# Pacing the modulation-weight chunks of a four-layer hybrid model: other breakpoints in the table that spreads them over the projection chunks

## Chip, cores and metric

One core of a Trainium2 chip runs the whole program. The metric is device time in microseconds (us) of one execution, and the median over several executions is what counts. The granted clock of TensorE (PE) has two levels, 1.2 and 2.4 GHz; the profile gives it as a share of the upper one.

## What is computed

Four layers act on a sequence of 256 tokens of width 2048. Each layer is modulated by a vector that depends only on `c`, and its weights are large: 2048 x 6144 floats per layer.

```python
c_act = jax.nn.silu(c)
for i in range(DEPTH):                      # 4 layers
    mod = jnp.einsum('bd,de->be', c_act, ada_w[i]) + ada_b[i]
    shift, scale, gate = jnp.split(mod[:, None, :], 3, axis=-1)
    h = rms_normalize(x, norm_g[i], NORM_EPS) * (1 + scale) + shift
    ...                                     # layers 0 and 3: rwkv7_mixer, 1: gla_mixer, 2: ssd_mixer
    x = x + (gate * out).astype(x.dtype)
return rms_normalize(x, final_g, NORM_EPS)
```

Each mixer is one wide input projection (cut into several parts), a recurrence over heads in chunks, and an output projection.

## The kernel before

**Projections.** All projections go through `jobs` (L359 and on). A projection of 256 output columns is cut into *weight chunks* of 512 KB (four 128-row slices of 256 columns; the output projection of a RWKV layer also has chunks of two slices). For each weight chunk SP issues one DMA into a tile `raw` (L348), ScalarE (ACT) casts it into `H` (L338), VectorE (DVE) subtracts to get the rest `L` (L340), and PE runs 24 matmuls of 256 columns with it (L393): high x high, high x low and low x high. After each weight chunk `tick()` is called.

**Modulation.** The first layer's shift and scale are made at the start. The other ten thirds (layer 0's gate, then shift, scale and gate of layers 1 to 3) are made by the generator `ada_third` in 320 *modulation chunks*, 32 to a third. Each is one DMA of 512 KB into a tile `raw` and one DVE operation of 128 x 1024 elements that multiplies and adds it into `adaacc` (L304). Both kinds of chunk share the six `raw` buffers and the SP queue: SP waits, in order, until a buffer is free.

**Pacing.** `tick()` counts the weight chunks (`tk`, 670 in all) and reads from the table `PACE` how many modulation chunks should have been asked for by now. It asks for at most two per tick. During the last column block of a layer's output projection, and the first jobs of the next layer, `hold` is set and none is asked for. Where a layer needs a third that isn't complete, `ada_need` asks for all that is missing at once.

```python
n = min(int(np.interp(self.tk, *PACE)), self.paced + 2)
if not self.hold:
    self.ada_tick(n - self.paced)
    self.paced = n
```

`tk` is 144 at the end of layer 0, 276 at the end of layer 1, 502 at the end of layer 2 and 670 at the end. Layer 1 can't start before 97 modulation chunks have been asked for, layer 2 before 193, layer 3 before 289.

**Order.** A scheduler places the instructions of each engine when the program is built; each engine then runs its own in that order. In a RWKV layer the stages are: V projection, K projection (with `rwkv_first` for eight units of heads: elementwise work and the inverse of small triangular blocks through `bd`, `dx`, `dt`, mostly on DVE), R projection (with `rwkv_second`), G projection, and the output projection in three parts: units 0 to 3, units 4 to 6, and unit 7, whose weight chunks are half as large. "Out 1" below are the first 24 weight chunks of it, "Out 2" the last 16.

Of the kernel before, what the change touches and what calls it, by code (L numbers as in the profile page):

```python
# [92 lines left out]

RAWC = 1024

PACE = ((0, 60, 78, 150, 319, 530, 660), (0, 0, 16, 96, 234, 292, 320))

SHARE = (1, 0, 1, 0, 1, 0, 1, 0)

# [30 lines left out]
class Kern:  # L130
# [264 lines left out]
    def tick(self):  # L395

        self.tk += 1
        n = min(int(np.interp(self.tk, *PACE)), self.paced + 2)
        if not self.hold:
# [1066 lines left out]
```

## Time and profile before

| | us |
|---|---|
| median of 3 runs | 2886.83 |
| lowest and highest run | 2881.13, 2887.49 |
| profiled execution | 2881.41 |
| its span, first to last instruction | 2879.4 |
| PE busy | 2691.4 |
| DVE busy | 2213.7 |
| ACT busy | 1392.7 |

A row of windows of the profile gives the busy time of each engine in a stretch of the execution; length minus busy time is the engine's idle time there. The stretches used below begin where ACT casts the first weight chunk of a stage:

| stage | us from the span's start |
|---|---|
| layer 0: K, R, G | 199.7, 340.6, 490.8 |
| layer 0: Out 1, Out 2 | 660.8, 805.1 |
| layer 1 (gla): its first 24 weight chunks, then the next 96 | 866.8, 963.3 to 1281.5 |
| layer 2 (ssd): group 0; group 1 to its gate part; to the end of the first output block | 1352.3, 1408.3, 1491.8 |
| layer 2: the next 56 weight chunks; the 56 after them | 1613.3, 1789.4 |
| end of layer 2 and start of layer 3 | 2042.2 to 2158.7 |
| layer 3: K, R, G | 2227.4, 2372.7, 2522.8 |
| layer 3: Out 1, Out 2 | 2695.6, 2823.4 to 2853.6 |

### The profile page before, as it was taken

To read this page: it belongs to the slowest core of one execution; us is meant where nothing else is said; L and a number is where in the kernel's file an instruction comes from. 1 tells how busy PE (TensorE), PEld (TensorE's weight loads), DVE (VectorE), ACT (ScalarE), POOL (GpSimd) and SP (SyncE) were. 2 spreads that over 40 slices of the span, in tenths; PEclk is the share of its full clock that TensorE was granted. 3 is DMA by queue.
4 is the path that set the end of the run, shared out by engine and by line. 5 is a ranking of instruction groups with operands and counts; after the bars stand their busy time and mean duration, and the time that the engine had idled before them with its cause. 6 is when DMAs were issued, how large, how long until landed. Compare 5 with 4: busy or idle time off the path is not lost.

```text
span 2879.4 us, 62022 instructions
## 1 busy us (share of the span) xinstructions
PE 2691.4 (93%) x25074; PEld 2533.2 (88%) x25074; DVE 2213.7 (77%) x3918; ACT 1392.7 (48%) x2315; POOL 153.8 (5%) x298
## 2 busy tenths in 40 slices
PE   6899899999977999998998999999889989999997
PEld 4789899998967899987898999999779989899997
DVE  5778777878788988877888787887678888565666
ACT  3475655333335544444544454554357666452333
POOL 0011110101000000000000000000001011110100
PEclk8899889999998999999999999999999989999999
DMA  9876558978586888975775767666557765684633
GB/s 341 313 239 198 165 162 285 352 270 293 178 287 222 315 296 295 321 257 196 280 264 191 233 221 232 220 212 223 180 170 242 228 197 184 194 299 160 206 118 114
DMA packets 239118, 673.55 MB, mean 234 GB/s; under 512 B 72272, under 2 KB 78416, under 8 KB 235760
## 3 DMA queue, kind: packets, MB, share of 16 engines
q1 hardware_dynamic: 217904, 580.84, 59.8%
q0 software_dynamic: 20928, 88.75, 8.6%
q8 instruction: 197, 3.23, 0.5%
q14 instruction: 89, 0.73, 0.1%
HBM read 620.66 MB, written 48.82 MB: 233 GB/s over the span
## 4 chain that ended last, share of the span: by engine, by line
PE 72%; DVE 10%; DMA 10%; issue 3%; ACT 2%; SPq 2%; POOL 0%; DVEq 0%; ACTq 0%; POOLq 0%
PE acc L393 56%; DMA raw<-in_ada_w 3%; DVE L L340 3%; PE g L785 2%; PE pv L393 2%; DVE adaacc L304 2%; ACT H L338 1%; DMA raw<-in_rwkv_w_in 1%; DMA raw<-in_rwkv_w_out 1%; DMA dx<-bd 1%; PE b L892 1%; PE b L869 1%; DMA raw<-in_gla_w_in 1%; PE b L891 1%; PE b L864 1%
## 5 line engine op out<-in xcount | busy, mean ns | idle before, releaser
L393 PE MATMUL acc<-xs,H 128*128 128x256 f32 x8480 | 1631.3, 291 | 32.0 <-ACT H L338 8.4
L393 PEld LDWEIGHTS acc<-xs,H 128*128 128x128 f32 x8480 | 1359.7, 196 | 61.7 <-ACT H L338 10.9
L393 PE MATMUL acc<-xs,L 128*128 128x256 f32 x4240 | 1228.9, 290 | 18.2 <-DVE L L340 17.9
L338 ACT CAST H<-raw 128x1024 fp32r<-128x1024 f32 (+1 forms) x706 | 718.2, 1018 | 862.0 <-PE acc L393 636.1
L340 DVE TENSOR_TENSOR L<-raw,H 128x1024 fp32r<-128x1024 f32 (+1 forms) x706 | 834.1, 1184 | 249.0 <-ACT H L338 233.9
L393 PEld LDWEIGHTS acc<-xs,L 128*128 128x128 f32 x4240 | 828.3, 195 | 31.9 <-DVE L L340 23.4
L304 DVE SCALAR_TENSOR_TENSOR adaacc<-raw,cact,adaacc 128x1024 f32<-128x1024 f32 x300 | 384.0, 1280 | 111.5 <-DMA raw<-in_ada_w 109.5
L393 PE MATMUL acc<-ys,H 128*128 128x256 f32 x1536 | 292.2, 290 | 10.1 <-DVE ys L409 3.8
L393 PEld LDWEIGHTS acc<-ys,H 128*128 128x128 f32 x1536 | 244.7, 194 | 20.7 <-issue 7.4
L393 PE MATMUL acc<-ys,L 128*128 128x256 f32 x768 | 221.1, 288 | 0.0
L393 PEld LDWEIGHTS acc<-ys,L 128*128 128x128 f32 x768 | 149.0, 194 | 3.2 <-issue 3.2
L551 ACT ACTIVATE hn<-x,mod,omu 128x256 f32<-128x256 f32 x192 | 113.4, 599 | 2.9 <-DVE xm L554 1.4
L431 DVE SCALAR_TENSOR_TENSOR x<-acc,mod,x 128x256 f32<-128x256 f32 x192 | 83.7, 478 | 33.3 <-PE acc L393 33.1
L393 PE MATMUL acc<-H,xs 128*128 128x256 f32 x512 | 97.4, 290 | 0.9 <-ACT vt L1072 0.7
L554 DVE SCALAR_TENSOR_TENSOR xm<-x,par,hn 128x256 f32<-128x256 f32 x192 | 88.9, 478 | 1.4 <-ACT hn L551 0.3
L393 PEld LDWEIGHTS acc<-H,xs 128*128 128x128 f32 x512 | 82.7, 198 | 2.5 <-issue 1.2
L393 PE MATMUL acc<-L,xs 128*128 128x256 f32 x256 | 73.7, 289 | 0.0
L785 PE MATMUL g<-abkp 64*128 64x128 f32 x768 | 68.6, 294 | 1.8 <-DVE abkp L807 1.7
L408 ACT CAST xs<-xm 128x256 fp32r<-128x256 f32 x128 | 50.9, 400 | 34.1 <-DVE xm L554 31.8
L785 PEld LDWEIGHTS g<-abkp 64*128 64x128 f32 x768 | 53.4, 189 | 14.2 <-issue 6.2
L1278 DVE SCALAR_TENSOR_TENSOR cva<-cvp,hcw,cva 128x256 f32<-128x256 f32 x144 | 65.1, 478 | 0.0
L278 DVE SCALAR_TENSOR_TENSOR adaacc<-raw,cact,adaacc 128x512 f32<-128x512 f32 x56 | 42.0, 749 | 28.1 <-DMA raw<-in_ada_w 23.4
(358 smaller groups left out, 3138.4 us busy)
## 6 DMA issues: line engine op xcount, KB each, us to landing
raw<-in_ada_w SPq DMA_DIRECT2D x384, 512.0 KB, 4.9
raw<-in_rwkv_w_in SPq DMA_DIRECT2D x256, 512.0 KB, 4.8
raw<-in_ssd_w_in SPq DMA_DIRECT2D x128, 512.0 KB, 4.3
raw<-in_gla_w_in SPq DMA_DIRECT2D x96, 512.0 KB, 5.2
raw<-in_ssd_w_out SPq DMA_DIRECT2D x64, 512.0 KB, 4.0
raw<-in_rwkv_w_out SPq DMA_DIRECT2D x48, 512.0 KB, 4.4
abkp<-kd POOLq DMA_DIRECT2D x16, 1024.0 KB, 7.8
raw<-in_gla_w_out SPq DMA_DIRECT2D x32, 512.0 KB, 4.9
```

Of the source, the lines that this page charges most:

```text
L278: nc.vector.scalar_tensor_tensor(out=acc, in0=raw[:, u, :], scalar=self.cact[:, k:k + 1], in1=acc, op0=ALU.mult, op1=ALU.add)
L304: nc.vector.scalar_tensor_tensor(out=acc, in0=raw, scalar=self.cact[:, k:k + 1], in1=acc, op0=ALU.mult, op1=ALU.add)
L338: nc.scalar.copy(out=hi, in_=raw[:, a:a + n])
L340: nc.vector.tensor_tensor(out=lo, in0=raw[:, a:a + n], in1=hi, op=ALU.subtract)
L393: self.nc.tensor.matmul(ps, lhs, rhs, start=first and part == 0 and w is hi, stop=last and w is lo)
L408: nc.scalar.copy(out=t[:, 0, :], in_=src)
L431: nc.vector.scalar_tensor_tensor(out=self.x[:, t, 1:], in0=ps[:, u, :], scalar=gate[:, t:t + 1], in1=self.x[:, t, 1:], op0=ALU.mult, op1=A ...
L551: nc.scalar.activation(t1, x[:, k, 1:], AF.Identity, scale=self.omu[:, col:col + 1], bias=self.mods[(i, 0)][:, k:k + 1])
L554: done[k] = nc.vector.scalar_tensor_tensor(out=xm, in0=x[:, k, 0:T], scalar=self.p("rwkv_mu", col), in1=t1, op0=ALU.mult, op1=ALU.add)
L785: self.nc.tensor.matmul(ps[h][:, n * C:(n + 1) * C], s[r, q, c * C:(c + 1) * C], t[r, q, c * C:(c + 1) * C], start=True, stop=True)
L864: nc.tensor.matmul(ps[:, n * H:(n + 1) * H], G[h][:, q, :], tk[:, 2, q, HS[h]], start=not c, stop=not c or h == 1)
L1278: nc.vector.scalar_tensor_tensor(out=a, in0=src[:, k:k + T], scalar=w[k], in1=a, op0=ALU.mult, op1=ALU.add)
```

## The change

Only the table is changed: its first tuple holds counts of weight chunks, the second the modulation chunks to be asked for by then.

```diff
-PACE = ((0, 60, 78, 150, 319, 530, 660), (0, 0, 16, 96, 234, 292, 320))
+PACE = ((0, 156, 286, 518, 640), (0, 97, 194, 290, 320))
```

The rate in modulation chunks per weight chunk goes from 0 (first 60), 0.89, 1.11, 0.82, 0.27 and 0.22 to 0.62, 0.75, 0.46 and 0.25. Counted in the order in which SP issues the loads of the two programs, the modulation chunks fall so:

| stage (weight chunks in it) | before | after |
|---|---|---|
| layer 0: V (40) | 1 | 5 |
| K (32) | 0 | 20 |
| R (32) | 10 | 20 |
| G (32) | 34 | 20 |
| Out 1 (24) | 27 | 15 |
| Out 2 (16), the forced ones at its end included | 25 | 17 |
| layer 1: first 24 | 22 | 17 |
| next 96 | 79 | 72 |
| last 16 | 12 | 12 |
| layer 2: group 0 and group 1 (16 + 24) | 33 | 19 |
| to the end of the first output block (32) | 9 | 17 |
| the next 56 and 56 and 24 | 15, 15, 7 | 23, 23, 10 |
| end of layer 2 and start of layer 3 (26) | 7 | 11 |
| layer 3: V, K, R, G | 5, 7, 7, 5 | 5, 8, 6, 0 |
| Out 1, Out 2 | 0, 0 | 0, 0 |

The SP queue of the program before, in layer 0 from the last two LoRA loads (`rwkv_dec_w`, `rwkv_iclr_w`) through V's last eight loads into K. `bd` and `dx` are the small transfers of the inverse.

```order
L348 DMA raw<-in_rwkv_dec_w 128x384
L348 DMA raw<-in_rwkv_iclr_w 128x384
L348 DMA raw<-in_rwkv_w_in 128x1024 x25
L924 DMA bd<-LT 16x8x16 x8
L348 DMA raw<-in_rwkv_w_in 128x1024
L927 DMA dx<-bd 64x256
```

The same place in the program after; `in_ada_w` are the modulation chunks.

```order
L348 DMA raw<-in_rwkv_w_in 128x1024 x2
L298 DMA raw<-in_ada_w 128x1024
L348 DMA raw<-in_rwkv_w_in 128x1024
L298 DMA raw<-in_ada_w 128x1024
L348 DMA raw<-in_rwkv_w_in 128x1024 x2
L298 DMA raw<-in_ada_w 128x1024
L348 DMA raw<-in_rwkv_w_in 128x1024 x2
```

Where SP issued 25 weight chunks in a row, it now issues a modulation chunk after every one or two of them.

DVE in the K stage of layer 0 in the program before (`xm` and `xs` are the mixed input of the next projection, `thd` and `abk` belong to `rwkv_first`):

```order
L340 TENSOR_TENSOR L<-raw,H 128x1024 x2
L752 TENSOR_TENSOR thd<-thd,abk 128x512
L754 SCALAR_TENSOR_TENSOR abk<-abk 128x512
L340 TENSOR_TENSOR L<-raw,H 128x1024
L756 SCALAR_TENSOR_TENSOR abk<-abk,bkk 128x256
L758 SCALAR_TENSOR_TENSOR abk<-abk,nkk,Pt 128x256
```

The same work of DVE in the program after:

```order
L304 SCALAR_TENSOR_TENSOR adaacc<-raw,cact,adaacc 128x1024
L340 TENSOR_TENSOR L<-raw,H 128x1024 x2
L752 TENSOR_TENSOR thd<-thd,abk 128x512
L754 SCALAR_TENSOR_TENSOR abk<-abk 128x512
L340 TENSOR_TENSOR L<-raw,H 128x1024
L745 TENSOR_SCALAR n_2538<-b_2533 128x8
L756 SCALAR_TENSOR_TENSOR abk<-abk,bkk 128x256
L758 SCALAR_TENSOR_TENSOR abk<-abk,nkk,Pt 128x256
L756 SCALAR_TENSOR_TENSOR abk<-abk,bkk 128x256
L758 SCALAR_TENSOR_TENSOR abk<-abk,nkk,Pt 128x256
L304 SCALAR_TENSOR_TENSOR adaacc<-raw,cact,adaacc 128x1024
```

The modulation operations (L304) now stand between the `L` of the weight chunks and the work of `rwkv_first`; before, this stage had none.

The SP queue at the end of layer 0's output projection, before (`128x512` are the half chunks of unit 7, `gla_low` is the first load of layer 1):

```order
L348 DMA raw<-in_rwkv_w_out 128x512
L298 DMA raw<-in_ada_w 128x1024 x2
L348 DMA raw<-in_rwkv_w_out 128x512
L298 DMA raw<-in_ada_w 128x1024
L348 DMA raw<-in_rwkv_w_out 128x512
L298 DMA raw<-in_ada_w 128x1024
L348 DMA raw<-in_rwkv_w_out 128x512
L298 DMA raw<-in_ada_w 128x1024 x8
L348 DMA raw<-in_gla_low 128x4x16
```

The same place after:

```order
L348 DMA raw<-in_rwkv_w_out 128x512 x2
L298 DMA raw<-in_ada_w 128x1024
L348 DMA raw<-in_rwkv_w_out 128x512
L298 DMA raw<-in_ada_w 128x1024
L348 DMA raw<-in_rwkv_w_out 128x512 x2
L298 DMA raw<-in_ada_w 128x1024
L348 DMA raw<-in_rwkv_w_out 128x512 x2
L298 DMA raw<-in_ada_w 128x1024 x8
L348 DMA raw<-in_gla_low 128x4x16
```

Fewer modulation chunks stand between the half chunks; the eight that layer 1 forces at the end stand there in both.

## Rows read from the trace of the kernel before

**Rows 1.** The page's head: span, and PE's busy time and share.

```profile
span 2879.4 us, 62022 instructions
...
PE 2691.4 (93%) x25074; PEld 2533.2 (88%) x25074; DVE 2213.7 (77%) x3918; ACT 1392.7 (48%) x2315; POOL 153.8 (5%) x298
```

**Rows 2.** The page's costliest groups, L304: busy us, mean ns of one, idle before.

```profile
L304 DVE SCALAR_TENSOR_TENSOR adaacc<-raw,cact,adaacc 128x1024 f32<-128x1024 f32 x300 | 384.0, 1280 | 111.5 <-DMA raw<-in_ada_w 109.5
```

**Rows 3.** Windows: V's end, K, R, G, Out 1, Out 2, layer 1's start.

```profile
core 0: us, PE busy (x) PEld busy (x) DVE busy (x) ACT busy (x) POOL busy (x), PEclk, DMA share, GB/s
...
150.00:200.00 50.00, 46.30 (x353) 44.70 (x353) 34.63 (x60) 36.02 (x66) 8.96 (x20) 0.93 0.69 232
...
199.70:340.60 140.90, 136.04 (x1509) 129.68 (x1507) 115.67 (x253) 90.88 (x177) 14.93 (x28) 0.98 0.61 190
340.60:490.80 150.20, 144.73 (x2120) 137.17 (x2121) 108.35 (x206) 83.96 (x159) 15.70 (x31) 0.92 0.64 208
490.80:660.80 170.00, 166.78 (x1542) 157.43 (x1541) 137.66 (x214) 65.71 (x106) 19.92 (x37) 1.00 0.87 314
660.80:805.10 144.30, 136.98 (x1182) 128.92 (x1181) 108.66 (x207) 44.88 (x76) 11.76 (x22) 0.96 0.66 228
805.10:866.80 61.70, 43.66 (x292) 34.79 (x292) 54.10 (x78) 20.89 (x40) 0.00 (x0) 0.95 0.87 289
866.80:963.30 96.50, 83.03 (x590) 74.87 (x591) 82.11 (x121) 54.44 (x83) 0.52 (x1) 0.88 0.71 238
```

**Rows 4.** Windows: layer 3's K, G, Out 1, Out 2.

```profile
2227.40:2372.70 145.30, 136.41 (x1358) 128.91 (x1357) 122.12 (x261) 92.90 (x181) 14.89 (x26) 0.95 0.68 220
...
2522.80:2695.60 172.80, 172.05 (x1701) 161.08 (x1700) 103.33 (x183) 65.42 (x108) 19.95 (x37) 1.00 0.63 217
2695.60:2823.40 127.80, 125.89 (x1126) 119.91 (x1125) 88.96 (x191) 43.44 (x74) 11.74 (x22) 1.00 0.49 160
2823.40:2853.60 30.20, 30.20 (x249) 29.03 (x247) 20.61 (x35) 14.19 (x23) 0.00 (x0) 1.00 0.36 119
```

**Rows 5.** Windows of L304 alone: layer 0's G, Out 1, Out 2; layer 3's K, G.

```profile
490.80:660.80 170.00, 42.23 (x33) 1.00 0.87 314
660.80:805.10 144.30, 25.59 (x20) 0.96 0.66 228
805.10:866.80 61.70, 29.43 (x23) 0.95 0.87 289
...
2227.40:2372.70 145.30, 7.68 (x6) 0.95 0.68 220
...
2522.80:2695.60 172.80, 5.10 (x4) 1.00 0.63 217
```

**Rows 6.** Windows of 72 us: in layer 0's G, and in layer 1.

```profile
504.00:576.00 72.00, 69.33 (x618) 65.39 (x616) 57.93 (x90) 26.01 (x41) 10.27 (x19) 1.00 0.96 352
...
936.00:1008.00 72.00, 69.58 (x553) 63.94 (x553) 64.93 (x87) 37.84 (x60) 0.00 (x0) 0.98 0.89 315
```

**Rows 7.** The longest wait in Out 2: us in total, times, longest.

```profile
ACT H L338 <- DMA raw<-in_rwkv_w_out: 25.2, 15, 3.9
```

**Rows 8.** The chain of work that ended last in Out 2, by line.

```profile
by line: DMA raw<-in_rwkv_w_out 33.9%; DVE adaacc L304 18.5%; issue 16.2%; DVE x L431 11.3%; DVE L L340 7.1%; DMA raw<-in_gla_low 5.8%; ACT H L338 5.8%; DVE ylast L680 1.1%; DVE rst L1042 0.3%; DVE ysq L902 0.2%; DVE rsv L1035 0.2%; DVE rst
```

**Rows 9.** Windows: layer 1's middle, layer 2's first stretches, one steady, its end.

```profile
963.30:1281.50 318.20, 311.33 (x2522) 296.04 (x2522) 259.35 (x335) 143.91 (x206) 0.00 (x0) 0.98 0.85 302
...
1352.30:1408.30 56.00, 51.42 (x394) 49.85 (x393) 49.02 (x83) 31.71 (x47) 1.66 (x3) 0.94 0.75 259
1408.30:1491.80 83.50, 79.19 (x658) 76.58 (x657) 74.29 (x128) 41.64 (x59) 0.53 (x1) 0.96 0.85 299
1491.80:1613.30 121.50, 110.02 (x905) 106.07 (x904) 94.96 (x180) 53.70 (x76) 1.06 (x2) 0.94 0.58 196
1613.30:1789.40 176.10, 176.10 (x1497) 172.43 (x1496) 147.25 (x265) 89.39 (x127) 1.06 (x2) 1.00 0.68 225
...
2042.20:2158.70 116.50, 96.69 (x668) 86.76 (x668) 78.33 (x150) 57.05 (x102) 6.87 (x10) 0.88 0.48 159
```

## The prediction

> **What bounds the kernel now.** I read the page first: PE is busy for 93% of the span and DVE for 77% [rows 1], so on the whole this is a PE kernel, and a modulation chunk, which costs no PE time, is free wherever PE has other work and DVE and the queues keep up. What it costs DVE is 1.280 us each [rows 2]; what it costs the DMA engines is 512 KB. Then I cut the span into the stages of the layers and read windows, each engine's busy time against the length. Three kinds of stage come out. In the steady part of layer 2 PE has no idle time at all, with DVE busy for 147.25 of 176.1 us, 0.84 [rows 9]. In the RWKV stages K and R PE is idle for 4.9 and 5.5 us and DVE is busy for 0.82 and 0.72 [rows 3]. And at the seams PE does stand still: 18.0 of 61.7 us in Out 2, 13.5 of 96.5 us at layer 1's start [rows 3], 4.6, 4.3 and 11.5 us in the first three stretches of layer 2 [rows 9], with the granted clock down to 0.88 to 0.96 there. The chain of waits in Out 2 tells what the standstill is made of: a third of it is weight chunks landing, 18.5% modulation operations on DVE [rows 8], and ACT waited 25.2 us for weights [rows 7]. So the question of this change is what 20 chunks cost where they go (K, which had none) against what 8 of them give back where they leave (Out 2), and a few smaller moves.
>
> **The change part by part.** It adds and removes no work: 320 chunks before and after. Each term is the number of chunks moved times a price from the nearest stage.
>
> *K, 20 chunks more.* DVE works 115.7 us in the 140.9 us of this stage [rows 3]; 20 x 1.280 = 25.6 us more makes 141.3 us, all of the stage. Nothing in the trace runs DVE at that: the fullest 72 us beside a nearly full PE has 64.93, 0.902 [rows 6]. At that share 141.3 us take 156.7, which is 15.8 us longer. A second price: the same stage in layer 3 ran 145.3 us with 6 chunks [rows 4, 5], 4.4 us longer, 0.73 us a chunk if all of it is theirs, and 20 of them 14.7. From below the bound is 0: if the chunks fell exactly into DVE's 25.2 idle us. From above it is 25.6, every operation on the path. I take +14, a little under the two prices, because part of this stage's DVE work, the block inverses, is first needed in R. A late `L` stops PE's next matmuls, and with them the cast of the next chunk; the small `bd` and `dx` transfers come later too, but what waits for them is `rwkv_second`, a stage on.
>
> *V's end, 4 more, and R, 10 more.* V's end has DVE at 34.6 of 50 us [rows 3], so 5 us fit. R's DVE goes from 108.4 to 121.2 of 150.2 us, 0.81, which is what G has now (137.7 of 170.0) with 3.2 us of PE idle [rows 3]. Cover: DVE's 41.9 idle us. +1, from 0 to +12.8 if the cover were gone.
>
> *G, 14 fewer.* It took 170.0 us while 33 chunks were worked in, and layer 3's G 172.8 with 4 [rows 3 to 5]: a price of nothing. 0, at best -3.2, its PE idle time.
>
> *Out 1, 12 fewer.* PE was idle for 7.3 us with 20 chunks worked in, and for 1.9 us in layer 3's with none [rows 3 to 5]: 5.4 / 20 x 12 = 3.2; the clock was 0.96 against 1.00. -4, from 0 to -6.
>
> *Out 2, 8 fewer.* 61.7 us with 23 chunks worked in, against 30.2 for the same 16 weight chunks in layer 3 with none [rows 3 to 5]: 31.5 / 23 = 1.37 us a chunk, 8 of them -11. Bounds: 0, if the standstill hangs on something else (below), and -18, all of PE's idle time there.
>
> *Layer 1's start, 5 fewer.* At most 5 x 1.280 = 6.4 us, at least nothing; PE's 13.5 idle us [rows 3] sit partly in the norm's own chain. -3. Its middle, 7 fewer: 6.9 us of PE idle in 318.2 [rows 9], so 0.
>
> *Layer 2's start, 14 fewer, then 8 more.* In the first two stretches DVE is at 0.88 and 0.89 and PE idle for 8.9 us together, with clocks of 0.94 and 0.96 [rows 9]: -4, from 0 to -9. In the third DVE rises from 95.0 by 10.2 to 105.2 of 121.5 us, 0.87, with 11.5 us of PE idle there already [rows 9]: +2, from 0 to +10.
>
> *The steady part of layer 2, 19 more in 80 + 56 weight chunks.* A period's DVE goes from 147.25 by 8 x 1.280 to 157.5 of 176.1 us, 0.89. The cover is now exactly full PE: no idle at all [rows 9]. Near 0.9 the second stretch of layer 2 loses 4.3 of 83.5 us, but it has no output projection beside it to fill PE. 0 to +10; +2.
>
> *The seam to layer 3, 4 more, and layer 3.* 4 x 1.280 = 5.1 us at most, where PE is idle for 19.8 of 116.5 us [rows 9]: +1. In layer 3 one more in K and 6 fewer in R and G: 0.
>
> Sum: 14 + 1 + 0 - 4 - 11 - 3 - 4 + 2 + 2 + 1 = -2 us. The profiled execution took 2881.4 us, 5.4 below the median of the runs, so I put the sum to the middle of the two, 2884: **2882 us**. Some 0.2% (5.8 us) is what a measurement of this kernel can tell from no change, and -2 is inside it.
>
> **A rule weighed against the trace.** Out 2 moved 289 GB/s [rows 3], while the same core had 352 in a stretch of G with PE running on [rows 6]. By bytes alone, then, Out 2 isn't at the limit, and its waits would be the landing time of each load behind a full set of `raw` buffers. The Trainium skill ("DMA: Bandwidth & Descriptors", Specifications) gives a core some 358 GB/s of HBM; the trace agrees as far as its fullest stretch, 352, goes. By that rule Out 2 has bandwidth to spare and gives nothing back.
>
> **The rivals.**
>
> *Even (the forecast).* K's loss and the seams' gains cancel to within 5.8 us. Against it: two terms of 14 and 11 us with wide bounds must come out close to each other.
>
> *K is hidden: faster.* G worked in 33 chunks with DVE at 0.81 and lost nothing [rows 3]; PE's own work fills 136.0 of K's 140.9 us, so if DVE's operations only slip behind each other and the inverses run over into R, K costs 0. Then -2 - 14 = -16, 2868 us. Every price of K under 10 us makes the kernel faster by more than 0.2%. Against it: G's DVE had 32 us left, K's would have none.
>
> *K and R are bound by DVE: slower.* DVE takes its operations in order; a chunk whose data hasn't landed (109.5 us of such waits in all [rows 2]) holds the `L` behind it, and there is no idle time left to absorb it. At full price K costs 25.6 and R 12.8, 23.4 more than I took: 2882 + 23 = 2905 us. It decides from K and R together at 23 us on. For it: the stage where DVE is fullest beside PE gets the largest addition. The Trainium skill ("TensorE: Matmul & The Clock Gate", Architectural detail) calls DVE a strict first-in, first-out engine; the waits just named agree.
>
> *Out 2 gives nothing back: slower.* By the waits on landing described above: 2882 + 11 = 2893 us. Against it: modulation operations stand on Out 2's chain themselves [rows 8], and layer 3's Out 2 without them took half as long [rows 4].
>
> **How the numbers follow.** Even 0.35; K hidden, or the seams giving more than I took, 0.33; K and R bound by DVE 0.25; Out 2 giving nothing 0.07. So faster 0.33, same 0.35, slower 0.32. The range from 2860 to 2906 takes in the three rivals' times and leaves out the combination of all upper or all lower bounds. The forecast's own range is 2876 to 2888.
>
> **What the profile of the changed kernel would show.** K right: its window is 150 to 160 us long, DVE at 0.9 or more in it, PE waiting for `L`. K hidden: 141 to 145 us. Out 2 right: 48 to 53 us, with ACT's wait for `rwkv_w_out` well under 25 us. Layer 2's periods still 176 us with PE idle near 0; if they grow to 180, the steady term was mis-sized. G unchanged at 170 us with its DMA share down from 0.87. The forecast is wrong if a seam I priced at nothing moves: the end of layer 1, or layer 3, where the schedule differs though the chunks hardly do. A reordering by the scheduler that costs PE time in stages without moved chunks would show there, and I have no price for it.

## The result and the profile after

The changed kernel takes 2928.72 us (median of 4 runs, 2923.57 to 2933.8) against 2885.12 for the kernel before (4 runs): a ratio of 1.0155, with a 95% interval of 1.013 to 1.0181. It is slower by 1.6%, some 44 us, where 2882 was forecast and 2906 was the upper end of the range. The kernel before was timed again beside each experiment below (medians of 2885 to 2889); the ratios go by those times.

The page of the changed kernel, its span, its busy line, the chain that ended last by line, and the group L304. They answer to [rows 1] and [rows 2].

```profile
span 2931.8 us, 61975 instructions
...
PE 2712.5 (93%) x25074; PEld 2549.5 (87%) x25074; DVE 2211.0 (75%) x3918; ACT 1396.3 (48%) x2315; POOL 154.5 (5%) x298
...
PE acc L393 51%; DMA raw<-in_ada_w 8%; DVE L L340 4%; PE g L785 2%; PE pv L393 2%; DVE adaacc L304 2%; DMA raw<-in_rwkv_w_in 1%; PE b L892 1%; DMA dx<-bd 1%; PE b L891 1%; PE b L869 1%; PE b L864 1%; ACT H L338 1%; DVE xm L554 1%; DMA bd<-LT 1%
...
L304 DVE SCALAR_TENSOR_TENSOR adaacc<-raw,cact,adaacc 128x1024 f32<-128x1024 f32 x300 | 384.0, 1280 | 213.6 <-DMA raw<-in_ada_w 209.9
```

The chain by line in the kernel before:

```profile
PE acc L393 56%; DMA raw<-in_ada_w 3%; DVE L L340 3%; PE g L785 2%; PE pv L393 2%; DVE adaacc L304 2%; ACT H L338 1%; DMA raw<-in_rwkv_w_in 1%; DMA raw<-in_rwkv_w_out 1%; DMA dx<-bd 1%; PE b L892 1%; PE b L869 1%; DMA raw<-in_gla_w_in 1%; PE b L891 1%; PE b L864 1%
```

The busy time of DVE is what it was, and each modulation operation still takes 1280 ns. What changed is the last pair of numbers: DVE now stands still for 209.9 us before these operations because the chunk hasn't landed, against 109.5 us in [rows 2]. And the landing of `in_ada_w` is now 8% of the chain that ended last, 3% before.

Windows of the changed kernel, with the columns of [rows 3]: K, R, G, Out 1, Out 2, layer 1's start and middle, layer 2's first three stretches, its steady part in three (56, 56 and 24 weight chunks), and the seam to layer 3.

```profile
206.30:357.80 151.50, 140.45 (x1453) 132.03 (x1452) 135.58 (x274) 93.17 (x182) 15.08 (x27) 0.97 0.75 246
357.80:509.10 151.30, 140.76 (x2106) 132.57 (x2107) 120.30 (x215) 85.14 (x157) 16.03 (x33) 0.94 0.72 238
509.10:663.30 154.20, 153.06 (x1469) 145.16 (x1467) 109.26 (x178) 61.82 (x98) 16.23 (x30) 1.00 0.79 278
663.30:824.30 161.00, 153.50 (x1288) 144.09 (x1288) 111.75 (x221) 46.96 (x80) 15.54 (x29) 0.93 0.57 194
824.30:868.60 44.30, 41.75 (x329) 36.23 (x327) 41.51 (x66) 20.65 (x40) 0.00 (x0) 1.00 0.82 279
868.60:955.80 87.20, 73.66 (x545) 69.23 (x546) 73.47 (x113) 48.87 (x71) 0.52 (x1) 0.86 0.70 235
955.80:1290.60 334.80, 320.61 (x2567) 303.92 (x2568) 256.74 (x336) 149.93 (x218) 0.00 (x0) 0.97 0.82 277
...
1361.20:1414.80 53.60, 49.72 (x393) 48.56 (x393) 45.49 (x77) 31.61 (x48) 1.66 (x3) 0.97 0.74 250
1414.80:1492.80 78.00, 77.48 (x663) 75.45 (x662) 70.29 (x132) 42.47 (x65) 0.53 (x1) 1.00 0.73 241
1492.80:1614.80 122.00, 109.04 (x901) 104.27 (x900) 94.86 (x173) 52.88 (x72) 1.06 (x2) 0.96 0.67 229
1614.80:1811.00 196.20, 183.17 (x1504) 176.62 (x1503) 154.94 (x272) 91.40 (x128) 1.06 (x2) 0.97 0.67 223
1811.00:1999.30 188.30, 181.25 (x1501) 176.09 (x1500) 155.18 (x273) 90.22 (x126) 0.53 (x1) 0.98 0.70 231
1999.30:2083.40 84.10, 79.56 (x660) 76.66 (x659) 65.68 (x109) 39.70 (x60) 0.00 (x0) 0.98 0.66 216
2083.40:2204.70 121.30, 97.96 (x671) 87.10 (x670) 83.16 (x154) 57.32 (x103) 6.88 (x10) 0.87 0.54 175
```

Put beside [rows 3] and [rows 9], the lengths give this table (us); every trace is cut at the casts of the same weight chunks. The two profiled executions lie 52.4 us apart, the medians 44. The last two columns are two of the experiments below: *placed* is the changed kernel with each modulation operation put behind the weight chunk that was asked for before it (`after_fifo`), *no wait* the one in which DVE doesn't read the loaded chunk (`after_held`).

| stage | forecast | before | after | change | placed | no wait |
|---|---|---|---|---|---|---|
| up to K | in R's | 199.7 | 206.3 | +6.6 | 203.1 | 203.0 |
| K | +14 | 140.9 | 151.5 | +10.6 | 137.3 | 133.9 |
| R | +1, with V's end | 150.2 | 151.3 | +1.1 | 161.8 | 170.8 |
| G and Out 1 | -4 | 314.3 | 315.2 | +0.9 | 314.2 | 327.5 |
| Out 2 | -11 | 61.7 | 44.3 | -17.4 | 45.1 | 48.4 |
| layer 1's start | -3 | 96.5 | 87.2 | -9.3 | 92.8 | 85.4 |
| layer 1's middle | 0 | 318.2 | 334.8 | **+16.6** | 326.1 | 323.3 |
| layer 1's last 16 chunks | none | 70.8 | 70.6 | -0.2 | 66.2 | 64.4 |
| layer 2, first three stretches | -2 | 261.0 | 253.6 | -7.4 | 241.5 | 248.0 |
| layer 2, steady part | +2 | 428.9 | 468.6 | **+39.7** | 441.1 | 443.1 |
| seam to layer 3 | +1 | 116.5 | 121.2 | +4.7 | 119.5 | 122.6 |
| layer 3 | 0 | 694.9 | 701.3 | +6.4 | 707.4 | 688.2 |

In this pair of traces the steady part of layer 2 alone nearly makes the loss, and layer 1's middle, which had 7 modulation chunks *fewer*, is the next. In both, PE was full or nearly so before: in the steady stretch of [rows 9] it had no idle time and a granted clock of 1.00, and so in the two stretches behind it:

```profile
1789.40:1964.70 175.30, 175.30 (x1496) 172.18 (x1495) 144.99 (x262) 89.67 (x126) 0.53 (x1) 1.00 0.68 221
1964.70:2042.20 77.50, 77.50 (x662) 75.25 (x661) 62.16 (x106) 39.50 (x61) 0.00 (x0) 1.00 0.68 221
```

Now it is idle for 13.0, 7.1 and 4.5 us in the three stretches, at clocks of 0.97 and 0.98. With the clock PE's busy time in the first of them rose too (183.17 us, 176.10 in [rows 9]).

The chain of the first steady stretch (56 weight chunks) by line, before, and then after:

```profile
by line: PE acc L393 92.5%; PE b L1364 1.2%; PE b L1360 1.2%; PE b L1342 1.0%; PE b L1362 1.0%; PE b L1350 1.0%; PE mx L310 0.6%; PE b L1308 0.5%; PE b L483 0.5%; PE b L1387 0.4%; PE mx L316 0.2%; PE b L1313 0.1%
```

```profile
by line: PE acc L393 67.1%; DMA raw<-in_ada_w 13.0%; DVE L L340 4.8%; issue 3.5%; DVE adaacc L304 1.4%; DVE M L1325 1.2%; PE b L1360 1.0%; PE b L1364 1.0%; PE b L1362 0.9%; PE b L1350 0.9%; DVE yv L1391 0.8%; PE mx L310 0.6%; PE b L1342 0.5
```

Before, no transfer and no DVE operation is on it. After, modulation chunks in flight are 13%, and `L` 4.8%. How a chunk that PE never reads gets onto PE's chain is seen in the timeline of the changed kernel, in the first steady stretch (start us, length us, engine and line; in brackets the idle time before, with what ended it), for DVE, SP's queue, ACT and PE:

```profile
1641.94 1.23 DVE L340 TENSOR_TENSOR L<-raw,H 128x1024 fp32r<-128x1024 f32 x1
1646.46 1.28 DVE L304 SCALAR_TENSOR_TENSOR adaacc<-raw,cact,adaacc 128x1024 f32<-128x1024 f32 x1 [3.29 <-DMA raw<-in_ada_w]
...
1648.16 1.23 DVE L340 TENSOR_TENSOR L<-raw,H 128x1024 fp32r<-128x1024 f32 x1
...
1641.67 0.33 SPq L298 DMA_DIRECT2D raw<-in_ada_w  x1
...
1643.07 1.05 ACT L338 CAST H<-raw 128x1024 fp32r<-128x1024 f32 x1 [1.16 <-issue]
...
1649.44 0.38 PE L393 MATMUL acc<-xs,L 128*128 128x256 f32 x1 [0.34 <-DVE L L340]
```

SP asks for the chunk at 1641.67. DVE reaches its operation when the `L` before it ends, at 1643.17, 1.5 us after that, and stands until 1646.46. Meanwhile ACT has cast the next weight chunk into `H` by 1644.12; its `L` could be made then, but it stands behind the modulation operation and three short ones, and starts at 1648.16, 4.0 us later. PE has other chunks' matmuls to work off and waits only 0.34 us for this one; over the whole stretch it waits for an `L` six times, 6.1 us together, where the trace of before has no wait of PE at all:

```profile
PE acc L393 <- DVE L L340: 6.1, 6, 2.2
```

(The Trainium skill, "TensorE: Matmul & The Clock Gate", Architectural detail, calls DVE's queue a strict first-in, first-out; this row agrees, since a ready `L` waited 4.0 us.)

The waits of DVE for modulation chunks (us in total, times, longest), before, in layer 1's middle and in the first and second steady stretch:

```profile
DVE adaacc L304 <- DMA raw<-in_ada_w: 8.0, 10, 1.7
...
DVE adaacc L304 <- DMA raw<-in_ada_w: 11.1, 9, 1.7
...
DVE adaacc L304 <- DMA raw<-in_ada_w: 14.0, 11, 2.9
```

The same three stretches after:

```profile
DVE adaacc L304 <- DMA raw<-in_ada_w: 39.7, 39, 2.9
...
DVE adaacc L304 <- DMA raw<-in_ada_w: 20.9, 11, 4.7
...
DVE adaacc L304 <- DMA raw<-in_ada_w: 19.1, 13, 2.5
```

Layer 1's middle has fewer chunks and five times the wait. Counted in the two traces, a modulation operation there stood ahead of the `L` of 0.93 weight chunks that SP had asked for earlier, on average, before, and of 2.15 after: with the sparser table the scheduler puts the operation nearer to the issue of its own load. (PE doesn't wait for `L` there; its longest wait is for `gth`, another operation of DVE's, 6.6 us.) In the steady part the operations stood 3.9 weight chunks ahead before and 3.5 after; there it is their number that grew.

### The profile page after: what moved, and what is told of

It is laid out like the page before. It is cut to its first block, busy times and chain, and to the rows that moved or that the text cites. A ratio compares the mean times of both kernels' runs of the same rounds, so it can differ in the third digit from the quotient of the medians.

```text
span 2931.8 us, 61975 instructions
## 1 busy us (share of the span) xinstructions
PE 2712.5 (93%) x25074; PEld 2549.5 (87%) x25074; DVE 2211.0 (75%) x3918; ACT 1396.3 (48%) x2315; POOL 154.5 (5%) x298
## 4 chain that ended last, share of the span: by engine, by line
PE 67%; DVE 13%; DMA 13%; issue 4%; ACT 1%; SPq 1%; POOL 0%; DVEq 0%; POOLq 0%; ACTq 0%
PE acc L393 51%; DMA raw<-in_ada_w 8%; DVE L L340 4%; PE g L785 2%; PE pv L393 2%; DVE adaacc L304 2%; DMA raw<-in_rwkv_w_in 1%; PE b L892 1%; DMA dx<-bd 1%; PE b L891 1%; PE b L869 1%; PE b L864 1%; ACT H L338 1%; DVE xm L554 1%; DMA bd<-LT 1%
## 5 line engine op out<-in xcount | busy, mean ns | idle before, releaser
L304 DVE SCALAR_TENSOR_TENSOR adaacc<-raw,cact,adaacc 128x1024 f32<-128x1024 f32 x300 | 384.0, 1280 | 213.6 <-DMA raw<-in_ada_w 209.9
L408 ACT CAST xs<-xm 128x256 fp32r<-128x256 f32 x128 | 50.8, 400 | 47.0 <-DVE xm L554 44.5
L841 ACT COPY tk<-b 128x256 f32<-128x256 f32 (+1 forms) x48 | 21.3, 443 | 91.3 <-PE b L839 51.8
```

The costliest lines, as they stand in the source:

```text
L304: nc.vector.scalar_tensor_tensor(out=acc, in0=raw, scalar=self.cact[:, k:k + 1], in1=acc, op0=ALU.mult, op1=ALU.add)
L408: nc.scalar.copy(out=t[:, 0, :], in_=src)
```

## The experiments

The theory: DVE's waiting for modulation chunks that haven't landed, with `L` queued behind, costs the 44 us. The rivals: the additional work itself fills DVE (the forecast's K and R, or the steady part); the even rate in layer 0 does it; and the place of the operations among DVE's others does it, whether they wait or not.

**`after_fifo`: the waits taken out of the changed kernel.** The scheduler is told to place each modulation operation behind the `L` of the weight chunk that was asked for just before it. This fixes an order within DVE; nothing is left out.

```diff
-    nc.vector.scalar_tensor_tensor(out=acc, in0=raw, scalar=self.cact[:, k:k + 1], in1=acc,
-                                   op0=ALU.mult, op1=ALU.add)
+    self.after(nc.vector.scalar_tensor_tensor(out=acc, in0=raw, scalar=self.cact[:, k:k + 1], in1=acc,
+                                   op0=ALU.mult, op1=ALU.add), self.last)
...
-        nc.vector.tensor_tensor(out=lo, in0=raw[:, a:a + n], in1=hi, op=ALU.subtract)
+        self.last = nc.vector.tensor_tensor(out=lo, in0=raw[:, a:a + n], in1=hi, op=ALU.subtract)
```

> The changed table, and each modulation operation on DVE placed behind the L of the weight chunk that was asked for just before it; nothing else. Theory A (DVE is held by chunks that have not landed): DVE's waits for in_ada_w fall from 209.9 us to under 100, the steady periods of layer 2 from 196.2 and 188.2 us to under 182, the whole to 2885 to 2905 us. Theory B (the work of the chunks themselves, 1.28 us each, fills DVE): periods stay above 185 us and the whole within 2920 to 2935. Theory C (only the scheduler's other order costs): any time, with no tie to DVE's waits for in_ada_w.

Measured: 2878.99 us, 0.9967 of before (0.9951 to 0.9983), and 50 us less than the changed kernel. Its page and two windows, the first two steady stretches:

```profile
L304 DVE SCALAR_TENSOR_TENSOR adaacc<-raw,cact,adaacc 128x1024 f32<-128x1024 f32 x300 | 382.9, 1276 | 4.5 <-DMA raw<-in_ada_w 2.7
...
1588.10:1771.30 183.20, 179.54 (x1504) 175.13 (x1504) 154.30 (x271) 90.64 (x129) 1.05 (x2) 0.98 0.71 239
1771.30:1953.60 182.30, 178.45 (x1500) 174.29 (x1499) 155.39 (x272) 89.44 (x125) 0.53 (x1) 0.99 0.71 235
```

The waits fall from 209.9 to 2.7 us at the same DVE work, and the two stretches from 196.2 and 188.3 to 183.2 and 182.3 us, just above the 182 below which the theory expected them, while the whole came out below its range. The additional work isn't the cause of most of the loss.

**`before_fifo`: the same edit in the kernel before.** It tells whether the table still matters once nothing waits.

> The old table with the same placing behind L. Theory A: DVE's waits for in_ada_w fall from 109.5 us to under 60; PE is already full in the steady parts, so the whole gains little, 2870 to 2885 us. Theory B: 2880 to 2890, no change. Theory C: any.

Measured: 2879.26 us, 0.9965 (0.9949 to 0.9982). With the operations placed, the two tables take 2879.0 and 2879.3: no difference. The waits of before cost it some 6 to 10 us (0.35%); those of after cost some 50.

**`l0_even_only` and `l2_old`: which part of the table.** The first has the new even rate up to the end of layer 0's 97 chunks and the old points from 319 on, with a rate of 0.84 in layer 1; the second also has the new rate in layer 1 (0.75) and catches up at the start of layer 2. Both have the old rate in the steady part.

```diff
-PACE = ((0, 60, 78, 150, 319, 530, 660), (0, 0, 16, 96, 234, 292, 320))
+PACE = ((0, 156, 319, 530, 660), (0, 97, 234, 292, 320))
...
-PACE = ((0, 60, 78, 150, 319, 530, 660), (0, 0, 16, 96, 234, 292, 320))
+PACE = ((0, 156, 286, 319, 530, 660), (0, 97, 194, 234, 292, 320))
```

> The changed table in layer 0 alone (0.62 a weight chunk), the old points from 319 on. By the two traces layer 0 ends 1.8 us later and the first 24 weight chunks of layer 1 take 9.3 us less: theories A and B expect 2875 to 2888 us. Theory C: the K stage and everything behind it is reordered, so a loss of 10 us or more is possible.

> The changed table in layers 0 and 1, then 40 chunks early in layer 2 and 0.27 a weight chunk after, as before. Theories A and B: the steady periods of layer 2 come back to 176 us each, some 40 us less than the changed kernel, against some 5 to 15 us lost at layer 2's start: 2890 to 2905 us. Theory C: 2915 or more.

Measured: `l0_even_only` 2881.85 us, 0.9974 (0.9958 to 0.9991); `l2_old` 2902.74, 1.005 (1.0027 to 1.0072). The even layer 0 costs nothing: its K takes 152.1 us, and Out 2 44.5, but the whole is a little faster than before. `l2_old` has layer 1's middle at 335.3 us, as the changed kernel has (334.8), and `l0_even_only` at 323.3. Its second stretch of layer 2, into which 26 modulation operations crowd, takes 100.1 us, where `l0_even_only` needs 78.4. In the steady part both have the old lengths, 176.0 and 175.6, and 176.0 and 176.3. So in these traces the loss sits in layer 1's rate and in the steady part. The total of the waits is not a price by itself: `l0_even_only` has 152.7 us of them, 43 more than before, and is no slower. About half of the 43 lie in layer 1's middle (27.7 us against 8.0), which takes 5.1 us longer.

**`after_lead2`, `after_lead3`: in doses.** The edit of `after_fifo`, but the operation may stand up to two, or up to three, weight chunks further ahead (`self.ls` lists the `L` so far, made where `self.last` was).

```diff
-    ..., self.last)
+    ..., self.ls[-3])
...
-    ..., self.last)
+    ..., self.ls[-4])
```

> The changed table, modulation operations at most two weight chunks ahead of their place in the queue (none: 2879 us; up to five, as the scheduler has it: 2929). Theory A: DVE's waits for in_ada_w fall to between 3 and 60 us, and the time follows them to 2880 to 2900. Theory A': halfway, 2900 to 2910, whatever the waits.

> The changed table, modulation operations at most three weight chunks ahead of their place. None 2879 us (DVE waits 2.7 us for in_ada_w), two 2882 (46.8), free 2929 (209.9). Theory A: the waits come out between 60 and 130 us and the time between 2885 and 2910, along the line of the other three. Theory A': a step of the same size from two to three as from three to free, whatever the waits.

| operation may stand ahead by | DVE's waits, us | time, us | ratio to before |
|---|---|---|---|
| 0 (`after_fifo`) | 2.7 | 2878.99 | 0.9967 (0.9951 to 0.9983) |
| up to 2 | 46.8 | 2881.8 | 0.998 (0.9959 to 1.0001) |
| up to 3 | 105.0 | 2897.55 | 1.0045 (1.0019 to 1.007) |
| free (the changed kernel) | 209.9 | 2928.72 | 1.0155 (1.013 to 1.0181) |

Waits and time rise together, slowly at first. With a lead of two, none of the waits lie in the steady part; that what is left is covered by the `L` that PE has in store is likely, but not shown.

**`after_resident`, then `after_held`: the place without the wait.** The operation may stand up to four weight chunks ahead, but it reads a constant in place of the loaded chunk. The chunk is still loaded; what is left out in both is the modulation itself, whose sum is of constants.

```diff
-    nc.vector.scalar_tensor_tensor(out=acc, in0=raw, scalar=self.cact[:, k:k + 1], in1=acc,
-                                   op0=ALU.mult, op1=ALU.add)
+    self.after(nc.vector.scalar_tensor_tensor(out=acc, in0=self.c("eps").broadcast_to([P, RAWC]),
+                                   scalar=self.cact[:, k:k + 1], in1=acc,
+                                   op0=ALU.mult, op1=ALU.add), self.ls[-5])
```

> The changed table; every modulation chunk is still loaded, but the operation on DVE reads a constant that is already there in place of the chunk (the modulation is left out), and may stand up to four weight chunks ahead of the L of the weight chunk asked for before it, as in the changed kernel. Theory A (DVE is held until the chunk lands): without that wait 2875 to 2895 us, steady periods of layer 2 near 180. Theory A' (the place alone costs: the chunk's work is done before older weight chunks' L): 2915 to 2935 us, as the changed kernel.

Measured: 2915.76 us, 1.0111 (1.007 to 1.0152). DVE waits for no chunk any more, and the time lies in the range that the rival (the place alone) gave. But the run decides nothing, for the wait went elsewhere. The waits of SP's queue for modulation chunks, in the changed kernel and then here:

```profile
SPq L348 <- DMA raw<-in_ada_w: 206.7, 119, 5.2
```

```profile
SPq L348 <- DMA raw<-in_ada_w: 622.1, 207, 7.7
...
ACT H L338 <- DMA raw<-in_gla_w_in: 50.0, 23, 3.7
```

Nobody reads the chunk now, so its buffer is given to the next weight chunk at once, and SP stands until the chunk that is still in flight into it has landed: 622.1 us. The weight chunks come late for that: ACT waits 50.0 us for those of layer 1, 16.6 in the changed kernel. `after_held` mends this: ACT reads one column of each chunk (into `ad1`, a tile of one column), behind the cast of the weight chunk that was asked for before it, so that the buffer stays taken until the chunk has landed.

```diff
-    ..., self.ls[-5])
+    ..., self.ls[-5]); self.after(nc.scalar.copy(out=self.ad1, in_=raw[:, 0:1]), self.hs)
...
-        nc.scalar.copy(out=hi, in_=raw[:, a:a + n])
+        self.hs = nc.scalar.copy(out=hi, in_=raw[:, a:a + n])
```

> As the run with the constant (the changed table, DVE reads a constant in place of the chunk, up to four weight chunks ahead; the modulation is left out), but each chunk's buffer stays taken until ACT has read one column of it, behind the cast of the weight chunk asked for before it; so SP no longer runs into a buffer whose chunk is still on its way. Theory A (waiting for the landing costs): 2875 to 2895 us. Theory A' (the place ahead of older L costs by itself): 2910 us or more, as with the constant before (2916).

Measured: 2883.53 us, 0.9985 (0.9963 to 1.0008). The page's group and the three steady stretches:

```profile
L304 DVE SCALAR_TENSOR_TENSOR adaacc<-cst,cact,adaacc 128x1024 f32<-128x1024 f32 x300 | 383.0, 1277 | 2.5 <-ACT adaacc L302 1.9
...
1604.60:1787.30 182.70, 178.64 (x1505) 174.01 (x1504) 154.20 (x270) 92.60 (x150) 1.05 (x2) 0.99 0.72 239
1787.30:1970.20 182.90, 179.33 (x1500) 174.37 (x1499) 155.55 (x274) 91.11 (x148) 0.53 (x1) 0.99 0.70 236
1970.20:2047.70 77.50, 77.50 (x660) 75.12 (x659) 65.40 (x109) 39.93 (x70) 0.00 (x0) 1.00 0.70 232
```

The operations are as many and as long, and they stand further ahead than in the changed kernel (of 3.4 weight chunks on average, against 2.6), yet 45 us are gone, although R takes 19.5 us longer than in the changed kernel, and G with Out 1 12.3 (perhaps for the reads added to ACT; that wasn't taken apart). 13 of the 45 lie in layer 3, which the order alone can move as much (below). The place ahead, without the wait, doesn't bring the loss: the rival had put it at 2910 us or more.

**`after_moved` and `after_moved_fifo`: the same at a neighbouring table.** All points lie one chunk earlier, but the last, which lies one later; first free, then with the edit of `after_fifo`.

```diff
-PACE = ((0, 156, 286, 518, 640), (0, 97, 194, 290, 320))
+PACE = ((0, 155, 285, 517, 641), (0, 97, 194, 290, 320))
```

> The changed table with its points moved by one weight chunk, (155, 285, 517, 641): the same chunks per stage but for one or two, and another order from the scheduler. It tells what reordering alone is worth: theories A and B 2920 to 2935 us; if it leaves that by 15 us or more, single stages can't be compared so closely.

> The changed table moved by one weight chunk, with each modulation operation behind its L. Without that placing 2945 us and 226.7 us of waits. Theory A: 2872 to 2886 us, as the changed table so placed. If the 16 us between the two tables stay, they are the scheduler's order of other work: 2890 to 2900.

Measured: 2945.46 us, 1.0205 (1.0171 to 1.024), with waits of 226.7 us; and 2900.54, 1.0048 (1.0029 to 1.0066), with 4.6. Taking the waits away gives 45 us here too. But both are slower than their neighbours, by 17 and 22 us, though the tables differ by one weight chunk in each point. The first lies 10 us above the range expected for it; the second came out where the expectation for "the scheduler's order" had it.

The neighbour also shows which stages the waits explain. All the runs together, without `after_resident`, whose waits went to SP (us; the waits are DVE's for modulation chunks, and PE's for `L`, in the stretch; "old" and "new" is the rate of the steady part; layer 1's middle has the new rate in `l2_old` and in the runs named `after`):

| run | steady part: rate, DVE's waits, PE's waits for `L` | its length | layer 1's middle: DVE's waits | its length |
|---|---|---|---|---|
| `before` | old, 29.6, 0 | 428.9 | 8.0 | 318.2 |
| `l0_even_only` | old, 28.4, 0.4 | 429.0 | 27.7 | 323.3 |
| `l2_old` | old, 33.6, 0 | 428.3 | 37.9 | 335.3 |
| `before_fifo` | old, 0, 0 | 430.8 | 0 | 319.2 |
| `l0_even_fifo` | old, 0, 0 | 430.8 | 0 | 323.7 |
| `l0_even_fifo_moved` | old, 0, 0 | 428.0 | 0 | 322.0 |
| `after_fifo` | new, 0, 0 | 441.1 | 0 | 326.1 |
| `after_moved_fifo` | new, 0, 0 | 449.7 | 0 | 325.4 |
| `after_held` | new, 0, 0 | 443.1 | 0 | 323.3 |
| `after_lead2` | new, 0, 0 | 447.2 | 15.8 | 324.3 |
| `after_lead3` | new, 16.1, 0.2 | 446.5 | 29.3 | 326.2 |
| `after` | new, 56.4, 13.0 | 468.6 | 39.7 | 334.8 |
| `after_moved` | new, 64.6, 10.8 | 452.7 | 47.3 | 340.7 |

PE waits for `L` in the steady part in the two free runs at the new rate alone. In layer 1's middle up to 29.3 us of waits go with at most 326.2 us, and 37.9 or more with 334.8 or more. But in the steady part `after_moved`, with more waits than the changed kernel, is 3 us longer than when placed, where the other pair gives 27.5: how much the waits cost there hangs on the order too.

**`l0_even_fifo` and `l0_even_fifo_moved`: a version that beats both kernels, and its neighbour.** The table of `l0_even_only` with the edit of `after_fifo`, and that with points moved by one or two chunks.

```diff
+PACE = ((0, 156, 319, 530, 660), (0, 97, 234, 292, 320))
...
+PACE = ((0, 157, 318, 529, 659), (0, 97, 234, 292, 320))
```

> The even table in layer 0, the old points behind it, and each modulation operation behind its L. By the stages of the runs so far: K near 137 us and Out 2 near 45 as in the changed table so placed, layer 2's steady part near 430 as with the old: theory A 2862 to 2876 us. If placing and table don't add, 2876 to 2884.

> The fastest so far (even in layer 0, old behind it, each operation behind its L: 2856 us) with its points moved by one weight chunk. If its lead over the other placed tables (2879) comes of the table: 2850 to 2864 us. If it comes of the scheduler's order: 2868 to 2885.

Measured: 2856.21 us, 0.9904 (0.9867 to 0.994), the fastest of the study; and 2884.02, 0.9989 (0.9968 to 1.0009). The first came out below the range expected for it. The 28 us between them are not the rate's: 24.8 of them lie in layer 3 (681.1 against 705.9 us), where the chunks of a stage differ by one at most. That the first is faster stands; how much of it is its table does not.

## Why the prediction was wrong

**The step that failed** is "the steady part of layer 2, 19 more ... 0 to +10; +2": it measured +39.7, and +23.8 with the neighbouring table. The chunks were priced at their busy time, 1.280 us, and DVE's idle time was taken as cover: 147.25 of 176.1 us busy, so 28.9 us free in a period [rows 9]. The runs show two things in its place.

First, that idle time is poor cover even where nothing waits for a chunk. In the four runs at the new rate without any such wait the steady part takes 441.1 to 449.7 us, in the six at the old rate 428.0 to 430.8: the work itself, 24 us of DVE's time, costs 10 to 22 us, where the term had 10 as its upper bound. DVE's idle time was waiting of other kinds too: in `after_fifo`, with the waits for modulation chunks gone and 7 us more of work in it, DVE is still idle for 28.9 of the 183.2 us of the first stretch, most of it before an `L`, for casts of ACT:

```profile
DVE L L340 <- ACT H L338: 20.2, 23, 1.7
```

Second, the chunks wait as well. Before, 11.1 us of the 28.9 were DVE standing before the very operations that were to be added, at no cost to PE; at the new rate the waits in the steady part go from 29.6 to 56.4 us, and PE waits for `L` there, 13.0 us, where it had no wait at all. With the waits taken away 27.5 of the 39.7 us come back (25.5 in `after_held`), but only 3.0 of the neighbour's 23.8. So both parts are shown, and their shares aren't. The row of waits was to be had in the trace of before; the mechanism was named, but only in a rival for K and R.

**Layer 1's middle, "7 fewer: ... so 0"**, measured +16.6. The number of chunks was the wrong measure: with fewer of them the scheduler moved each nearer to its load, and the waits went from 8.0 to 39.7 us. `after_fifo` and `after_held` give back 8.7 and 11.5 us of it, and placing gives back 15.3 at the neighbouring table.

**K, +14**, measured +10.6, with DVE busy for 135.58 of 151.5 us, near the 0.9 of the step, and PE idle for 11.1 us (4.9 before). But the chunks needn't cost K that: in `after_fifo` it takes 137.3 us with as many chunks, less than before; R then takes longer, and K and R together 299.1 us, against 291.1 before and 302.8 after. As the rival "K is hidden" had it, the work slips into R, at a price of 8 us for both. The rival's time of 2868 supposed the rest of the sum.

**Out 2, -11**: right in sign, and too small against the -17.4 measured. Its price was read from windows that don't match: layer 0's ends with the first cast of layer 1, layer 3's with its own last cast. From first to last cast layer 0 took 48.9 us and layer 3 30.3, so 18.6 / 23 x 8 = 6.5 us was to be had from that reading; 14.9 came back. PE's 18.0 idle us there [rows 3] went down to 2.6; ACT's wait for `rwkv_w_out` [rows 7] is not among the longest there any more. "Out 2 gives nothing back" falls; the stage moved 279 GB/s, 289 before [rows 3], so bandwidth was to spare, as the rule weighed there says, but that did not keep it from gaining. **Layer 1's start**, -3, measured -9.3, and layer 2's first three stretches, -2, measured -7.4: both right in sign. G was to stay at 170 us and took 154.2, with Out 1 16.7 longer: small matmuls of `rwkv_second` went from the one to the other (PE's count falls by 73 and rises by 106), and the pair is even.

**The sum of the work, -2, is what the placed pair shows** (2879.0 against 2879.3), but not by its terms. Between those two traces K and R together lengthen by 8.6 us, the steady part by 10.3, and layer 1's middle and layer 3 by 6.9 each; Out 2 shortens by 13.5, layer 1's start by 11.1 and layer 2's first stretches by 11.5. That the sum fits is in part luck.

**What stays open.** Layer 3 took 6.4 us longer in the changed kernel and 12.5 in `after_fifo`, where one modulation chunk more or less can't be the reason; over all the traces it takes 681 to 707 us. The prediction named such a reordering, without a price. In near-identical tables, which differ by 17 to 28 us, the scheduler puts PE's and DVE's instructions in another order; which piece of the order costs that wasn't taken apart. Two pairs (50 and 45 us) and `after_held` (45) put the waits at about the whole loss of 44 us, but each of them also compares two orders, so their share is known no closer than those 17 to 28 us.

## What to carry to other kernels

An engine's idle time is not free room: here 24 us of work, put beside some 75 us of DVE's idle time in the steady part, cost 10 to 22 us even with no wait of its own, and more with it. Before pricing an added operation at its busy time or at nothing, read what the engine's idle time is spent waiting for, the operations of its own kind first. Where an in-order engine serves both the critical stream and a background one, tie the background operation to the place of its load in the queue (here 2929 to 2879 us) rather than leave it to a scheduler's guess of when the load lands. And run a table's neighbour before believing its gain: tables that differ by a chunk or two were up to 1% apart here.

## What the runs showed that was not expected

- A buffer whose contents nobody reads is not free: in `after_resident` SP's queue stood 622.1 us on chunks still in flight into buffers that had been given on, 206.7 in the changed kernel.
- DVE's total of waits can rise from 109.5 to 152.7 us (`l0_even_only`) and the kernel become slightly faster. In the second steady stretch of `after_moved` 22.2 us of waits went with 182.5 us, and `after_fifo`, without any, took 182.3.
- Fewer chunks of background work (79 to 72 in layer 1's middle) made a stage 5% longer.
